# Sums of weight quarters on another engine, two products placed earlier, and the norm's scale applied on token rows

## The chip, the cores and the metric

The kernel runs as one program on one core of a Trainium2 chip. The metric is the device time of one execution in microseconds (us); before the change it is the median of three runs. The core has a matrix engine (TensorE, PE, whose weight loads are the row PEld), a vector engine (DVE), a scalar engine (ACT), GpSimd (POOL) and an engine that here only issues transfers (SyncE, SP). Transfers are DMAs; those issued by POOL stand in POOL's own instruction order, and an *accumulating* DMA adds what it moves to what the target holds.

## What is computed

The reference is a backbone of two layers that share their structure. Each layer has a feed-forward block, a mixer and a second feed-forward block, each between a norm that is scaled and shifted by a conditioning vector and a norm that is gated:

```python
def _layer(x, mod, lp, ctx):
    s0, c0, g0, s1, c1, g1, s2, c2, g2 = jnp.split(mod, N_MOD, axis=-1)
    h = _rms(x, lp["g_pre"][0]) * (1 + c0) + s0
    f = _swiglu(h, lp["w_ffn_gate"][0], lp["w_ffn_up"][0], lp["w_ffn_down"][0])
    x = x + 0.5 * g0 * _rms(f, lp["g_post"][0])
    ...

def _swiglu(h, wg, wu, wd):
    return (jax.nn.silu(h @ wg) * (h @ wu)) @ wd
```

The part left out is the mixer with `s1`, `c1`, `g1` and the second feed-forward block (FFN) with `s2`, `c2`, `g2`. `_rms(x, g)` is `x * rsqrt(mean(x*x) + 1e-6) * g`. There are 640 tokens (128 context, 512 latent) of width 1024; context and latent tokens have conditioning vectors of their own. The hidden width is 2816. Everything is float32.

## The kernel before

The 640 tokens are five tiles `t` of 128. A float32 matmul is made of three products of split operands: a weight slab `raw` is cast to `whi` by ACT (`split`, line 105) and the rest `wlo` is a subtraction on DVE (line 106); the three are `whi` by `hi`, `whi` by `lo`, `wlo` by `hi`. Up to six pairs `whi`, `wlo` exist at a time, so the splits can run that many products ahead of PE.

The blocks run in the order FFN, mixer, FFN, FFN, mixer, FFN. The first two FFNs are plain, the last two are *paired*: the gate and up matrices of a slab of hidden units are multiplied by a scheme with seven instead of eight block products. `seven` does this for one matrix of 1024 columns `w_pair`, in quarters `a11`, `a12`, `a21`, `a22` of 128x512. It loads `x` (`a11`, `a12`), `s` and `y` (`a21`, `a22`) by three DMAs on SP, adds `a22` to `s` and `a11` to `a21` by two accumulating DMAs from DRAM, and runs seven products of 12 matmuls each, 128x128 by 128x320, in line 671: B11, B21, T1, T3, T2, B22, T4. Between them `a11 += s` (after B11 has used `a11`) and `a12 += a11` (after B21 has used `a12`) are made by two more accumulating DMAs, from SBUF to SBUF; all four are issued by POOL in line 656. T2 and B22 read those sums. Two sets of buffers let the next `seven` load while one runs. A paired FFN starts with eight-product work on operands of `h` that are ready first, and then calls `seven` 20 times; `combine4` makes the last sum of quarters of `h`, an operand of T4, between the two.

Between two blocks the tokens are finished tile by tile: `postnorm` adds the gated output to `x`, `prenorm` computes `n = x * rs` (`rs` the reciprocal root mean square, a POOL power in line 304), `turn` transposes `n` on PE (line 334) and applies the affine map with the columns `A` and `B` as it leaves PSUM, half the pieces on DVE and half on ACT, and splits it. `rows` brings the gate row `G` onto all partitions: it transposes 16 rows on PE, writes them to DRAM (`gd`) and reads them back by four broadcasting DMAs into `P` tiles of 128x512. The transitions into the mixers and into the second plain FFN (three) have a plain target, the others a paired one.

A scheduler that simulates the engines' timelines sets the order of instructions on each engine from dependences and the order of the code; tiles of pools are given back when their last reader is through.

Of the kernel before, what the change touches and what calls it, by code (L numbers as in the profile page):

```python
# [2 lines left out]

# [30 lines left out]
class Builder:  # L34
# [227 lines left out]

    def rows(self, pg, f, pn):
        nc, v = self.nc, self.nc.vector
        s = self.tmp.tile([P, 512], F32, tag="tmp", name=self.nm("rows"))[:, :16]
# [4 lines left out]
        out = {}  # L272
        if pn:
            l, ph = pn
            a = self.sm.tile([P, 2, 8], F32, tag="acol", name=self.nm("acol"), bufs=2)
            for c in range(2):
                v.scalar_tensor_tensor(out=a[:, c], in0=self.mod[l]["m"][c][:, (3 * ph + 1) * 8:(3 * ph + 2) * 8],
                                       scalar=1.0, in1=self.mod[l]["gpre"][:, ph * 8:ph * 8 + 8], op0=ALU.add, op1=ALU.mult)
            out["A"] = [a[:, c] for c in range(2)]
            out["B"] = [self.mod[l]["m"][c][:, 24 * ph:24 * ph + 8] for c in range(2)]  # L280
        ps = self.tr()
        nc.tensor.transpose(ps[:16, :P], s, self.ident)
        g = self.tmp.tile([32, P], F32, tag="tmp", name=self.nm("grow"))
        nc.scalar.copy(g[:16], ps[:16, :P])  # L284
        d = self.dr.tile([2, 1024], F32, tag=self.nm("gd"), name=self.nm("gd"))
        nc.gpsimd.dma_start(d.rearrange("c (k p) -> (c k) p", p=P), g[:16])  # L286
        out["G"] = []
        for c in range(2):
            w = [self.P_(shape=[P, 512]) for _ in range(2)]
            for h in range(2):  # L290
                nc.gpsimd.dma_start(w[h], d[c:c + 1, 512 * h:512 * h + 512].to_broadcast([P, 512]))
            out["G"].append(w)
        return out


# [12 lines left out]

    def prenorm(self, t, x, R, hT):
        nc, v = self.nc, self.nc.vector  # L310
        n = self.bg.tile([P, 1024], F32, tag="bg", name=self.nm("n"))
        ss = self.S_()
        sq = nc.scalar.activation(n, x, AF.Square, scale=1.0 / 32.0, accum_out=ss)
        rs = self.rstd(ss)
        self.norm = (v.tensor_scalar(n, x, rs, None, ALU.mult), sq)

        def turn():
            self.turn(t, n, R, hT)

        (self.turns if t < 3 else self.late).append(turn)  # L320

# [4 lines left out]

    def turn(self, t, n, R, hT):
        nc, v = self.nc, self.nc.vector
        a, b = (R[k][0 if t == 0 else 1] for k in "AB")
        hs = []  # L330
        for q in range(2):
            ps = self.tr()
            for i in range(4):
                nc.tensor.transpose(ps[:, i * P:(i + 1) * P], n[:, (4 * q + i) * P:(4 * q + i + 1) * P], self.ident)
            h = n[:, q * 512:(q + 1) * 512].rearrange("p (k t) -> p k t", k=4)
            for i in range(4):
                k = slice(4 * q + i, 4 * q + i + 1)
# [6 lines left out]
            if not hT.paired:  # L344
                hi, lo = (z[q][:, :, t * P:(t + 1) * P] for z in hT.raw)
                d = self.split(hi, lo, h)
        if hT.paired:
            for c, n_, half, o in self.PIECES[t]:
                h, cs = [h[:, :, c:c + n_] for h in hs], slice(o, o + n_)
                d = self.quarters(hT, h, half, cs)  # L350
                if half:
                    self.todo.append(lambda h=h, cs=cs: self.combine(hT, h, cs))
            if t == 2:
                self.combos()
        if t < 3:
            self.turned = d

# [106 lines left out]
    def ffn(self, l, i, hT, ph, nxt, last, first=None):  # L464
        nc, A = self.nc, self.A
# [5 lines left out]
        for ch, n in enumerate(phases):  # L471
# [8 lines left out]
            for nh in range(2):  # L480
                ps = [self.mm() for _ in range(NT)]
                STG = min(n - 1, self.stage(self.STG[0], hTn)) if (final and nh == 1) else 0
                for jj in range(n - STG):
                    if last and final and nh == 0 and jj == 1:
                        w = self.W_()
                        self.xpre = [self.xp.tile([P, 1024], F32, tag="x", name=self.nm("x")) for _ in range(2)] + \
                            [self.bg.tile([P, 1024], F32, tag="bg", name=self.nm("x")) for _ in range(2)] + [w[:, :1024]]
                        for t in range(NT):
                            nc.sync.dma_start(self.xpre[t], self.xsrc[t])
                    if dram and final and nh == 0 and jj == 0:  # L490
                        part = self.new_part()
                        for t in range(NT):
                            nc.gpsimd.dma_start(part[t].whole, self.pd[t])
                    if final and nh == 0 and jj == 3:
                        R = self.rows((l, ph), 0.5, None if last else nxt)
# [77 lines left out]
    def paired(self, l, i, hT):  # L573
# [3 lines left out]
        w, ps = {}, {}  # L577
# [31 lines left out]
        for f in range(2):  # L609
# [1 line left out]
            first(f, 1, 1)  # L611
            product(f, 1)
            self.combos()
        self.combine4(hT)
        st = [self.rawp.tile([P, 1024], F32, tag="raw", name=self.nm("raw")) for _ in range(2)] + [self.P_(shape=[P, 512])]
        extra = self.seven(W[0, 1], st, hT.t)
        next(extra)
        yield hid[0]
        yield hid[1]
        big = self.big.tile([P, 5120], F32, tag="big", name=self.nm("raw2"))  # L620
        sets = [[big[:, o:o + 1024], big[:, o + 1024:o + 2048], big[:, o + 2048:o + 2560]] for o in (0, 2560)]
        for jp in range(1, NJ // 2):
            hid = [(self.P_(F32R), self.P_(F32R)) for _ in range(2)]
            for m in range(2):
                self.background(4 * jp + 2 * m)
                if extra:
                    g, extra = extra, None
                else:
                    g = self.seven(W[m, jp], sets[m], hT.t)
                    next(g)  # L630
                out = next(g)
                for done in g:
# [16 lines left out]

    def seven(self, src, st, T):
        nc, v, g = self.nc, self.nc.vector, self.nc.gpsimd
        x, y, s = st
        a11, a12, a21, a22 = x[:, :512], x[:, 512:], y[:, :512], y[:, 512:]
        add = lambda o, a: g.dma_start(o, a, accum_op=ALU.add)  # L656
        nc.sync.dma_start(x, src[:, :1024])
        nc.sync.dma_start(s, src[:, 1024:1536])
        self.last_slab = nc.sync.dma_start(y, src[:, 1024:])
# [15 lines left out]
        pa, pb = self.mm(), self.mm()  # L675
        product(pa, a11, "B11")
        nc.scalar.copy(o[0][0], pa[:, :TH])  # L677
        add(a11, s)
        product(pb, a12, "B21")
        v.tensor_tensor(o[0][0], o[0][0], pb[:, :TH], ALU.add)  # L680
        add(a12, a11)
        yield [(0, 0)]
        pe, pf = self.mm(), self.mm()
        product(pe, s, "T1")
# [286 lines left out]
    def mixer(self, l, hT):  # L971
# [31 lines left out]
        for nh in range(2):  # L1003
            ps = [self.mm() for _ in range(NT)]
            STG = self.stage(self.STG[1], hTn) if nh else 0
            for kc in range(KC - STG):
                if nh == 0 and kc == 2:
                    R = self.rows((l, 1), 1.0, (l, 2))
# [681 lines left out]
```

## Time and profile before

| | |
|---|---|
| median of three runs | 3324.78 us (3321.77 to 3325.75) |
| the profiled execution | 3323.45 us, span 3321.7 us |
| mean granted TensorE clock | 0.966 |
| PE, PEld busy | 94%, 87% of the span |
| DVE, ACT, POOL busy | 63%, 42%, 25% |
| DMA traffic | 466.04 MB, mean 140 GB/s |

The span is the time from the first to the last instruction in the trace of one execution; the execution's own time is 1.75 us more. Busy means that an instruction runs on an engine; instructions that issue a DMA, wait or branch are not counted as busy, except on POOL where issuing is shown. The clock is what the chip granted TensorE, as a share of the full 2.4 GHz; its other level is 1.2 GHz.

### The profile page before, as it was taken

What the parts mean: (1) busy time and instruction counts of PE and PEld (TensorE: products, weight loads), DVE (VectorE), ACT (ScalarE), POOL (GpSimd) and SP (SyncE); (2) the same over time, 40 slices, a digit from 0 to 9 for tenths busy, and PEclk for the clock granted to TensorE, in tenths of its full rate; (3) what the DMA queues carried; (4) which work ended last, traced back from release to release, by engine and by line L of the source; (5) the groups of instructions that cost most, each with busy time, mean ns of one, the idle gap of its engine ahead of it and who ended that gap; (6) DMA issues with size and microseconds to landing.
All of it is one profiled execution on the core that took longest, in us unless ns stands there. A gap on an engine that the chain in (4) does not pass through costs nothing. (4 is left out here: it accounts for less than half of the span.)

```text
span 3321.7 us, 51922 instructions
## 1 busy us (share of the span) xinstructions
PE 3105.8 (94%) x19501; PEld 2880.7 (87%) x19501; DVE 2088.2 (63%) x4256; ACT 1380.7 (42%) x3066; POOL 832.1 (25%) x1156
## 2 busy tenths in 40 slices
PE   8889999999999989999979898989999998898988
PEld 6888997888999889989778888877989997788887
DVE  7993775656544496737676745567575865755455
ACT  4222224565543343322343333446664334444333
POOL 2640002039520054210111112110693101112121
PEclk9999999999999999999989899999999999899999
DMA  6364544422542334655456767534226634566663
GB/s 240 124 207 128 164 147 135 100 70 61 113 133 76 122 115 151 195 130 180 139 161 187 183 161 158 165 110 90 69 66 163 198 107 143 146 185 155 161 150 127
DMA packets 174396, 466.04 MB, mean 140 GB/s; under 512 B 39120, under 2 KB 47840, under 8 KB 173120
## 3 DMA queue, kind: packets, MB, share of 16 engines
q1 hardware_dynamic: 131712, 369.71, 36.2%
q0 software_dynamic: 41712, 91.70, 12.9%
q8 instruction: 153, 2.51, 0.3%
q10 hardware_dynamic: 720, 1.31, 0.1%
q14 instruction: 99, 0.81, 0.1%
HBM read 386.70 MB, written 60.09 MB: 135 GB/s over the span
## 5 line engine op out<-in xcount | busy, mean ns | idle before, releaser
L106 DVE TENSOR_TENSOR wlo<-raw,whi 128x512 fp32r<-128x512 f32 x901 | 642.3, 720 | 639.1 <-ACT whi L105 630.5
L105 ACT CAST whi<-raw 128x512 fp32r<-128x512 f32 x901 | 544.5, 618 | 888.1 <-PE mm L100 352.7
L98 PE MATMUL mm<-h,whi 128*128 128x256 f32 (+1 forms) x2560 | 796.1, 313 | 7.2 <-ACT h L105 4.5
L100 PE MATMUL mm<-h,wlo 128*128 128x256 f32 (+1 forms) x2560 | 794.5, 311 | 5.0 <-DVE wlo L106 4.9
L99 PE MATMUL mm<-h,whi 128*128 128x256 f32 (+1 forms) x2560 | 795.3, 311 | 0.0
L98 PEld LDWEIGHTS mm<-h,whi 128*128 128x128 f32 x2560 | 488.6, 191 | 12.2 <-ACT h L105 4.9
L100 PEld LDWEIGHTS mm<-h,wlo 128*128 128x128 f32 x2560 | 489.3, 191 | 7.0 <-DVE wlo L106 6.9
L99 PEld LDWEIGHTS mm<-h,whi 128*128 128x128 f32 x2560 | 489.9, 191 | 1.8 <-issue 1.2
L99 PE MATMUL mm<-wlo,P 128*128 128x512 f32 x1015 | 395.9, 391 | 0.0
L98 PE MATMUL mm<-whi,P 128*128 128x512 f32 x1015 | 393.9, 391 | 1.8 <-DVE tmp L562 1.8
L100 PE MATMUL mm<-whi,P 128*128 128x512 f32 x1015 | 395.3, 390 | 0.0
L259 DVE SCALAR_TENSOR_TENSOR junk<-wmod,srows 128x1024 bf16<-128x1024 f32 x256 | 317.1, 1239 | 77.7 <-DMA wmod<-w_mod 76.5
L671 PE MATMUL mm<-hT,whi 128*128 128x320 f32 x1280 | 300.1, 324 | 55.5 <-ACT P L677 34.4
L671 PEld LDWEIGHTS mm<-hT,whi 128*128 128x128 f32 x1280 | 225.0, 199 | 63.3 <-ACT P L677 39.3
L671 PE MATMUL mm<-hB,whi 128*128 128x320 f32 x960 | 231.4, 331 | 33.4 <-ACT whi L105 31.6
L98 PEld LDWEIGHTS mm<-whi,P 128*128 128x128 f32 x1015 | 191.2, 188 | 42.1 <-DVE tmp L562 2.3
L100 PEld LDWEIGHTS mm<-whi,P 128*128 128x128 f32 x1015 | 191.2, 188 | 39.8
L99 PEld LDWEIGHTS mm<-wlo,P 128*128 128x128 f32 x1015 | 191.3, 188 | 39.3 <-DVE wlo L106 0.5
L671 PEld LDWEIGHTS mm<-hB,whi 128*128 128x128 f32 x960 | 173.1, 204 | 42.9 <-ACT whi L105 37.1
L671 PE MATMUL mm<-hT,wlo 128*128 128x320 f32 x640 | 203.0, 320 | 0.0
L286 POOL DMA_DIRECT2D gd<-grow x6 | 3.0, 506 | 673.2 <-ACT grow L284 673.2
L105 ACT CAST P<-tmp 128x384 fp32r<-128x384 f32 (+1 forms) x112 | 51.6, 461 | 283.9 <-DVE tmp L563 269.8
(394 smaller groups left out, 5489.9 us busy)
## 6 DMA issues: line engine op xcount, KB each, us to landing
wmod<-w_mod SPq DMA_DIRECT2D x128, 512.0 KB, 4.2
raw<-w_down SPq DMA_DIRECT2D x88, 512.0 KB, 3.7
raw<-w_pair SPq DMA_DIRECT2D x88, 512.0 KB, 5.4
raw<-w_in_fm SPq DMA_DIRECT2D x72, 512.0 KB, 3.6
raw<-w_gate SPq DMA_DIRECT2D x44, 512.0 KB, 3.7
raw<-w_up SPq DMA_DIRECT2D x44, 512.0 KB, 3.6
raw<-w_pair POOLq DMA_DIRECT2D x78, 256.0 KB, 4.3
raw<-raw POOLq DMA_DIRECT2D x78, 256.0 KB, 5.2
```

What stands on the lines that cost most here:

```text
L98: nc.tensor.matmul(ps, whi, ahi, start=first, stop=False)
L99: nc.tensor.matmul(ps, whi, alo, start=False, stop=False)
L100: nc.tensor.matmul(ps, wlo, ahi, start=False, stop=last)
L105: nc.scalar.copy(hi, src)
L106: return nc.vector.tensor_tensor(lo, src, hi.bitcast(F32), ALU.subtract)
L259: nc.vector.scalar_tensor_tensor(out=jk, in0=w, scalar=1.0, in1=rows[:, c], op0=ALU.mult, op1=ALU.mult, accum_out=m[:, c:c + 1])
L286: nc.gpsimd.dma_start(d.rearrange("c (k p) -> (c k) p", p=P), g[:16])
L671: nc.tensor.matmul(ps[:, :TH], w[:, cs], T[b][:, z, k], start=not more and k == e == 0, stop=k == 3 and e == 2, skip_group_check=more)
```

## The change

Three things change. First, in `seven` the two sums between the products become additions on POOL (`addp`); the two sums from DRAM stay DMAs. Second, the generator of the first `seven` of a paired FFN is advanced past its first two products before `combine4` is written, so that their code stands ahead of it. Third, for a plain target `rows` also turns the scale `A` into a token row: one transpose of 32 rows and one broadcasting DMA of 1 MB each for `G` and `A`, into `W` tiles; `prenorm` then applies `rs` and `A` to the token tile (DVE the first half; ACT `rs` and POOL `A` the second half), and the new `turn_plain` only adds `B`: for the first two tiles one DVE addition of four pieces and then the split; for the others ACT writes the high part with a bias and DVE the low part. The last FFN, which has no following block, has only `G` there.

```diff
     def rows(self, pg, f, pn, paired):
...
+            if paired:
+                a = self.sm.tile([P, 2, 8], F32, tag="acol", name=self.nm("acol"), bufs=2)
+                out["A"] = a = [a[:, c] for c in range(2)]
+            else:
+                n, a = 32, [s[:, 16 + 8 * c:24 + 8 * c] for c in range(2)]
...
+        nc.gpsimd.dma_start(d.rearrange("c (k p) -> (c k) p", p=P)[:n], g[:n])
+        if paired:
...
+        for key, r in (("G", 0), ("A", 2))[:2 if pn else 1]:
+            w = self.W_()
+            nc.gpsimd.dma_start(w[:, 0:2048], d[r:r + 2].rearrange("c x -> (c x)").unsqueeze(0).to_broadcast([P, 2048]))
+            out[key] = [[w[:, 1024 * i + 512 * h:1024 * i + 512 * h + 512] for h in range(2)] for i in range(2)]
         return out
...
-        self.norm = (v.tensor_scalar(n, x, rs, None, ALU.mult), sq)
+        if hT.paired:
+            self.norm = (v.tensor_scalar(n, x, rs, None, ALU.mult), sq)
+        else:
+            a = R["A"][0 if t == 0 else 1]
+            self.norm = (
+                v.scalar_tensor_tensor(out=n[:, :512], in0=x[:, :512], scalar=rs, in1=a[0], op0=ALU.mult, op1=ALU.mult),
+                nc.scalar.mul(n[:, 512:], x[:, 512:], rs))
+            self.last_n = nc.gpsimd.tensor_tensor(n[:, 512:], n[:, 512:], a[1], ALU.mult)
...
+    def turn_plain(self, t, n, R, hT):
...
+            if t < 2:
+                h = n[:, q * 512:(q + 1) * 512].rearrange("p (k t) -> p k t", k=4)
+                v.tensor_tensor(h, ps.rearrange("p (k t) -> p k t", k=4),
+                                B[:, 4 * q:4 * q + 4].unsqueeze(2).to_broadcast([P, 4, P]), ALU.add)
                 d = self.split(hi, lo, h)
...
+            for i in range(4):
+                o, b = ps[:, i * P:(i + 1) * P], B[:, 4 * q + i:4 * q + i + 1]
+                nc.scalar.activation(hi[:, i], o, AF.Identity, bias=b)
+                d = v.scalar_tensor_tensor(out=lo[:, i], in0=o, scalar=b, in1=hi[:, i].bitcast(F32),
+                                           op0=ALU.add, op1=ALU.subtract)
...
-        self.combine4(hT)
         st = [self.rawp.tile([P, 1024], F32, tag="raw", name=self.nm("raw")) for _ in range(2)] + [self.P_(shape=[P, 512])]
         extra = self.seven(W[0, 1], st, hT.t)
         next(extra)
+        extra = extra, next(extra), [next(extra)]
+        self.combine4(hT)
...
+        addp = lambda o, a: g.tensor_tensor(o, o, a, ALU.add)
...
-        add(a11, s)
+        addp(a11, s)
         product(pb, a12, "B21")
         v.tensor_tensor(o[0][0], o[0][0], pb[:, :TH], ALU.add)
-        add(a12, a11)
+        addp(a12, a11)
```

Where the instructions now stand shows in three places. The first is SP's order around the loads of the first `seven` in the first paired FFN: `P` is the tile of `s`, `raw` those of `x` and `y`, `wmod` weights of the conditioning, `w_down` of the FFN's second matrix. Before:

```order
L659 DMA raw_2709_17303<-w_pair 128x1024
L657 DMA raw_17295<-w_pair 128x1024
L659 DMA raw_17296<-w_pair 128x1024
L255 DMA wmod_17906<-w_mod 128x1024
L255 DMA wmod_17928<-w_mod 128x1024
L658 DMA P_17297<-w_pair 128x512
L255 DMA wmod_17960<-w_mod 128x1024
```

and now:

```order
L700 DMA raw_2711_17353<-w_pair 128x512
L701 DMA raw_2711_17353<-w_pair 128x1024
L699 DMA raw_17292<-w_pair 128x1024
L701 DMA raw_17293<-w_pair 128x1024
L700 DMA P_17294<-w_pair 128x512
L256 DMA wmod_17916<-w_mod 128x1024
L78 DMA raw_17906<-w_down 128x1024
```

The load of `s` has moved ahead of the two `wmod` loads that it followed. The second is POOL's order in the first `seven`s of the same FFN, before:

```order
L656 DMA raw_17296<-w_pair 128x512
L656 DMA P_17297<-w_pair 128x512
L656 DMA raw_17295<-P_17297 128x512
L656 DMA raw_17295<-raw_17295 128x512
L656 DMA raw_2709_17303<-raw_2709_17303 128x512 x2
L656 DMA raw_2709_17303<-w_pair 128x512
L656 DMA raw_2709_17303<-raw_2709_17303 128x512
L656 DMA raw_2709_17303<-w_pair 128x512
```

and now:

```order
L697 DMA raw_17293<-w_pair 128x512
L697 DMA P_17294<-w_pair 128x512
L698 TENSOR_TENSOR raw_17292<-raw_17292,P_17294 128x512
L698 TENSOR_TENSOR raw_17292<-raw_17292 128x512
L698 TENSOR_TENSOR raw_2711_17353<-raw_2711_17353 128x512 x2
L697 DMA raw_2711_17353<-w_pair 128x512
L698 TENSOR_TENSOR raw_2711_17353<-raw_2711_17353 128x512
L697 DMA raw_2711_17353<-w_pair 128x512
```

The DMAs whose source is SBUF have become additions in the same places; those from `w_pair` have stayed. The third is POOL's order at the first transition (FFN to mixer), where `s` are the `rs` of a tile, `x` the sum into the residual. Before:

```order
L304 TENSOR_TENSOR s_5143<-s_5141,mhalf 128x1
L304 TENSOR_TENSOR s_5153<-s_5151,mhalf 128x1
L304 TENSOR_TENSOR s_5188<-s_5186,mhalf 128x1
L304 TENSOR_TENSOR s_5198<-s_5196,mhalf 128x1
L304 TENSOR_TENSOR s_5255<-s_5253,mhalf 128x1
L454 TENSOR_TENSOR x_5251<-part_2606,x_5251 128x512
L304 TENSOR_TENSOR s_5266<-s_5264,mhalf 128x1
L304 TENSOR_TENSOR s_5323<-s_5321,mhalf 128x1
L454 TENSOR_TENSOR x_5319<-part_2606,x_5319 128x512
```

and now:

```order
L315 TENSOR_TENSOR s_5138<-s_5136,mhalf 128x1
L315 TENSOR_TENSOR s_5148<-s_5146,mhalf 128x1
L315 TENSOR_TENSOR s_5185<-s_5183,mhalf 128x1
L333 TENSOR_TENSOR n_5143<-n_5143,W_4827 128x512
L315 TENSOR_TENSOR s_5195<-s_5193,mhalf 128x1
L333 TENSOR_TENSOR n_5190<-n_5190,W_4827 128x512
L315 TENSOR_TENSOR s_5248<-s_5246,mhalf 128x1
L492 TENSOR_TENSOR x_5244<-part_2606,x_5244 128x512
L315 TENSOR_TENSOR s_5259<-s_5257,mhalf 128x1
L315 TENSOR_TENSOR s_5312<-s_5310,mhalf 128x1
L333 TENSOR_TENSOR n_5254<-n_5254,W_4827 128x512
L492 TENSOR_TENSOR x_5308<-part_2606,x_5308 128x512
```

A multiply of `n` by the scale row `W` now stands among the powers and the sums for `x`, once for each token tile.

## Rows read from the trace of the kernel before

**Rows 1.** The page, engines and costliest group: busy us, share, instructions; group: busy, mean ns.

```profile
PE 3105.8 (94%) x19501; PEld 2880.7 (87%) x19501; DVE 2088.2 (63%) x4256; ACT 1380.7 (42%) x3066; POOL 832.1 (25%) x1156
...
L106 DVE TENSOR_TENSOR wlo<-raw,whi 128x512 fp32r<-128x512 f32 x901 | 642.3, 720 | 639.1 <-ACT whi L105 630.5
```

**Rows 2.** Waits of PE, whole span: us in total, times, longest.

```profile
PE mm L671 <- ACT whi L105: 50.8, 20, 7.4
PE mm L671 <- ACT P L677: 34.4, 17, 3.9
PE mm L334 <- DVE n L315: 29.8, 6, 8.8
```

**Rows 3.** Windows, six stretches of `seven`: us, then busy (instructions) by engine, PEclk, DMA.

```profile
1701.50:1771.70 70.20, 53.48 (x314) 51.58 (x313) 50.55 (x99) 26.38 (x56) 12.09 (x14) 0.85 0.63 155
1816.50:1941.30 124.80, 107.83 (x649) 102.47 (x648) 84.10 (x172) 51.72 (x113) 26.21 (x32) 0.92 0.74 179
1999.40:2120.50 121.10, 104.72 (x648) 101.61 (x647) 72.97 (x149) 53.35 (x117) 28.64 (x35) 0.93 0.64 140
2850.80:2916.40 65.60, 52.25 (x314) 50.17 (x313) 43.46 (x83) 26.99 (x57) 12.22 (x14) 0.87 0.58 135
2960.90:3078.80 117.90, 102.92 (x648) 100.13 (x647) 72.25 (x145) 51.40 (x114) 26.09 (x31) 0.95 0.73 170
3138.00:3255.10 117.10, 102.90 (x649) 100.17 (x648) 66.76 (x134) 52.00 (x115) 26.87 (x34) 0.94 0.68 157
sum 616.70, PE 524.11 PEld 506.13 DVE 390.10 ACT 261.84 POOL 132.13; mean PE 87.35 PEld 84.36 DVE 65.02 ACT 43.64 POOL 22.02
```

**Rows 4.** Windows, line 671 alone, a stretch without a stall.

```profile
2961.00:2982.00 21.00, 21.00 (x144) 20.90 (x143) 1.00 0.87 241
```

**Rows 5.** Waits of ACT, whole span: us in total, times, longest.

```profile
ACT whi L105 <- DMA raw<-raw: 234.3, 60, 7.5
```

**Rows 6.** The page, DMA issues: count, KB each, median us to landing.

```profile
raw<-w_pair POOLq DMA_DIRECT2D x78, 256.0 KB, 4.3
raw<-raw POOLq DMA_DIRECT2D x78, 256.0 KB, 5.2
```

**Rows 7.** Timeline of POOL and ACT in one `seven`: start, us, instruction, [idle before <-releaser].

```profile
2012.12 0.86 POOL L656 DMA_DIRECT2D raw<-raw  x1 [1.38 <-DVE wlo L106]
...
2020.18 0.86 POOL L656 DMA_DIRECT2D raw<-raw  x1
...
2019.76 0.62 ACT L105 CAST whi<-raw 128x512 fp32r<-128x512 f32 x1 [3.64 <-DMA raw<-raw]
...
2026.76 0.62 ACT L105 CAST whi<-raw 128x512 fp32r<-128x512 f32 x1 [6.01 <-DMA raw<-raw]
```

**Rows 8.** Timeline of SP and POOL at the last sum of h.

```profile
1701.87 0.38 SPq L658 DMA_DIRECT2D P<-w_pair  x1
...
1707.49 0.86 POOL L656 DMA_DIRECT2D P<-w_pair  x1 [14.15 <-DMA P<-w_pair]
```

**Rows 9.** Waits of PE, 1701.5 to 1716.5 and 2850.8 to 2863.

```profile
PE mm L671 <- ACT whi L105: 9.7, 2, 7.4
...
PE mm L671 <- ACT whi L105: 6.7, 1, 6.7
```

**Rows 10.** Line 454's group (ns min/median/max), then POOL and DVE timelines beside it.

```profile
L454 POOL TENSOR_TENSOR x<-part,x x15: 1264/1391/3938, 540.3 to 2816.7; 128x512 f32<-128x512 f32 x15
...
551.33 3.94 POOL L454 TENSOR_TENSOR x<-part,x 128x512 f32<-128x512 f32 x1 [0.83 <-ACT part L453]
...
552.24 1.29 DVE L106 TENSOR_TENSOR wlo<-raw,whi 128x512 fp32r<-128x512 f32 x2
...
2176.16 1.79 DVE L106 TENSOR_TENSOR wlo<-raw,whi 128x512 fp32r<-128x512 f32 x1
```

**Rows 11.** Groups of lines 315 and 453: ns min/median/max.

```profile
L315 DVE TENSOR_SCALAR n<-x,s x25: 744/753/755, 533.4 to 2826.9; 128x1024 f32<-128x1024 f32 x25
...
L453 ACT ACTIVATE part<-part,s x15: 722/723/750, 539.5 to 2815.9; 128x512 f32<-128x512 f32 x15
```

More of the change, by code (lines that the diff above doesn't have):

```diff
@@ L261, in mod_tile, with rows @@
         nc.vector.tensor_tensor(m, m, self.mod[l]["b"][:, col:col + 1].to_broadcast([P, 2]), ALU.add)
-    def rows(self, pg, f, pn):
+    def rows(self, pg, f, pn, paired):
         nc, v = self.nc, self.nc.vector
-        s = self.tmp.tile([P, 512], F32, tag="tmp", name=self.nm("rows"))[:, :16]
+        s = self.tmp.tile([P, 512], F32, tag="tmp", name=self.nm("rows"))[:, :32]
         l, ph = pg
@@ L272, in rows @@
         out = {}
+        n = 16
         if pn:
             l, ph = pn
-            a = self.sm.tile([P, 2, 8], F32, tag="acol", name=self.nm("acol"), bufs=2)
+            if paired:
[3 more added lines that the diff above has]
+                n, a = 32, [s[:, 16 + 8 * c:24 + 8 * c] for c in range(2)]
             for c in range(2):
-                v.scalar_tensor_tensor(out=a[:, c], in0=self.mod[l]["m"][c][:, (3 * ph + 1) * 8:(3 * ph + 2) * 8],
+                v.scalar_tensor_tensor(out=a[c], in0=self.mod[l]["m"][c][:, (3 * ph + 1) * 8:(3 * ph + 2) * 8],
@@ L278, in rows @@
                                        scalar=1.0, in1=self.mod[l]["gpre"][:, ph * 8:ph * 8 + 8], op0=ALU.add, op1=ALU.mult)
-            out["A"] = [a[:, c] for c in range(2)]
             out["B"] = [self.mod[l]["m"][c][:, 24 * ph:24 * ph + 8] for c in range(2)]
         ps = self.tr()
-        nc.tensor.transpose(ps[:16, :P], s, self.ident)
+        nc.tensor.transpose(ps[:n, :P], s[:, :n], self.ident)
         g = self.tmp.tile([32, P], F32, tag="tmp", name=self.nm("grow"))
-        nc.scalar.copy(g[:16], ps[:16, :P])
@@ L285, in rows @@
[L285 to L292, printed above, removed]
+        nc.scalar.copy(g[:n], ps[:n, :P])
+        d = self.dr.tile([4, 1024], F32, tag=self.nm("gd"), name=self.nm("gd"))
@@ new lines, in rows @@
+        nc.gpsimd.dma_start(d.rearrange("c (k p) -> (c k) p", p=P)[:n], g[:n])
+        if paired:
+            out["G"] = []
+            for c in range(2):
+                w = [self.P_(shape=[P, 512]) for _ in range(2)]
+                for h in range(2):
+                    nc.gpsimd.dma_start(w[h], d[c:c + 1, 512 * h:512 * h + 512].to_broadcast([P, 512]))
+                out["G"].append(w)
+            return out
+        for key, r in (("G", 0), ("A", 2))[:2 if pn else 1]:
+            w = self.W_()
+            nc.gpsimd.dma_start(w[:, 0:2048], d[r:r + 2].rearrange("c x -> (c x)").unsqueeze(0).to_broadcast([P, 2048]))
+            out[key] = [[w[:, 1024 * i + 512 * h:1024 * i + 512 * h + 512] for h in range(2)] for i in range(2)]
@@ L314, in prenorm @@
         rs = self.rstd(ss)
-        self.norm = (v.tensor_scalar(n, x, rs, None, ALU.mult), sq)
+        if hT.paired:
[6 more added lines that the diff above has]
+            self.last_n = nc.gpsimd.tensor_tensor(n[:, 512:], n[:, 512:], a[1], ALU.mult)
         def turn():
-            self.turn(t, n, R, hT)
+            (self.turn if hT.paired else self.turn_plain)(t, n, R, hT)
         (self.turns if t < 3 else self.late).append(turn)
@@ L343, in turn @@
             hs.append(h)
-            if not hT.paired:
-                hi, lo = (z[q][:, :, t * P:(t + 1) * P] for z in hT.raw)
-                d = self.split(hi, lo, h)
[L347 to L354, printed above, removed]
+        for c, n_, half, o in self.PIECES[t]:
+            h, cs = [h[:, :, c:c + n_] for h in hs], slice(o, o + n_)
+            d = self.quarters(hT, h, half, cs)
+            if half:
+                self.todo.append(lambda h=h, cs=cs: self.combine(hT, h, cs))
+        if t == 2:
+            self.combos()
+        if t < 3:
+            self.turned = d
+    def turn_plain(self, t, n, R, hT):
+        nc, v = self.nc, self.nc.vector
+        B = R["B"][0 if t == 0 else 1]
+        for q in range(2):
+            ps = self.tr()
+            for i in range(4):
+                kc = 4 * q + i
+                nc.tensor.transpose(ps[:, i * P:(i + 1) * P], n[:, kc * P:(kc + 1) * P], self.ident)
+            hi, lo = (z[q][:, :, t * P:(t + 1) * P] for z in hT.raw)
+            if t < 2:
+                h = n[:, q * 512:(q + 1) * 512].rearrange("p (k t) -> p k t", k=4)
+                v.tensor_tensor(h, ps.rearrange("p (k t) -> p k t", k=4),
+                                B[:, 4 * q:4 * q + 4].unsqueeze(2).to_broadcast([P, 4, P]), ALU.add)
+                d = self.split(hi, lo, h)
+                continue
+            for i in range(4):
+                o, b = ps[:, i * P:(i + 1) * P], B[:, 4 * q + i:4 * q + i + 1]
+                nc.scalar.activation(hi[:, i], o, AF.Identity, bias=b)
+                d = v.scalar_tensor_tensor(out=lo[:, i], in0=o, scalar=b, in1=hi[:, i].bitcast(F32),
+                                           op0=ALU.add, op1=ALU.subtract)
         if t < 3:
@@ L494, in ffn @@
                     if final and nh == 0 and jj == 3:
-                        R = self.rows((l, ph), 0.5, None if last else nxt)
+                        R = self.rows((l, ph), 0.5, None if last else nxt, not last and hTn.paired)
                     whi, wlo = next(it)
@@ L626, in paired @@
                 if extra:
-                    g, extra = extra, None
+                    g, out, head = extra
+                    extra = None
                 else:
-                    g = self.seven(W[m, jp], sets[m], hT.t)
+                    g, head = self.seven(W[m, jp], sets[m], hT.t), []
                     next(g)
-                out = next(g)
-                for done in g:
+                    out = next(g)
+                for done in itertools.chain(head, g):
                     for f, h in done:
@@ L1007, in mixer @@
                 if nh == 0 and kc == 2:
-                    R = self.rows((l, 1), 1.0, (l, 2))
+                    R = self.rows((l, 1), 1.0, (l, 2), hTn.paired)
                 whi, wlo = next(it)
```

1 line of the change is left out of this document (added).

## Prediction, written before the changed kernel ran

> **What bounds the kernel now.** I read the page first: TensorE (PE) is busy 3105.8 of 3321.7 us [rows 1]. What can be won is its idle time and the time in which its clock is low. The waits of PE say where the idle time lies: in line 671, the matmuls of the paired matrices' products, and at the turns of the normed tokens [rows 2]. So I cut out the six stretches in which the products of `seven` run and read them as windows [rows 3]: 616.70 us, PE busy 524.11, idle 92.6. At the full clock 144 such matmuls take 21.0 us [rows 4], 0.1458 us each, so 12 of a product take 1.75 us and the 84 of one `seven` 12.25. The 3222 matmuls of the stretches [rows 3] would take 469.8 us; that PE is busy 524.1 there, at a granted clock of 0.85 to 0.95 [rows 3], is 54.3 us for the lower of the two levels, 1.2 GHz, to which the clock drops around the stalls. Idle and clock together, 147 us, is the most that the stretches can give.
>
> What ends the idle time: ACT's casts of `whi` wait 234.3 us, 60 times, for the DMA that adds SBUF to SBUF [rows 5]. One `seven` shows how [rows 7]: POOL issues `a11+=s` at 2012.12 and the cast that reads it starts at 2019.76, 7.6 us later; `a12+=a11` is issued at 2020.18 and its cast starts at 2026.76, 6.6 us later. The median landing of such a DMA is 5.2 us [rows 6]. The two sums in series make 14.2 us, and PE wants the next operands every 12.25 us: 1.95 us are missing for each of the 38.4 `seven`s of the stretches (3222/84), 75 us. The idle time agrees: 92.6, less 9.7 and 6.7 us that stand at another place (below), is 76.2.
>
> **The change, part by part.** *The two sums on POOL.* It removes two DMAs from each `seven` (78 in the page [rows 6], two more under another name) and adds as many POOL additions 128x512. POOL runs that form already, in line 454: 1264 at least, 1391 median, 3938 ns at most [rows 10]. Two in series are 2.8 us at the median, and 7.9 us at the worst. Both ends lie under 12.25 us, so the chain that made PE wait is gone for either price; before it, POOL waits for the accumulating DMA `s+=a22`, which lands in 4.3 us [rows 6]: 0.86 us issue [rows 7] + 4.3 + 2.8 = 8.0 us, still under 12.25. What is late next: the first operands of a stretch, the loads of the sets, DVE's `wlo`. I have no row that shows these waits without the DMA; between 0 and the whole 76.2 I take a third, 26 us, as an estimate: six stretch starts of about 3 us, and single stalls of the size that remain beside the DMA. That is -50 us. Removing the stalls also removes drops of the clock. I scale the 54.3 us with the idle time.
>
> What the additions cost elsewhere: DVE shares the time with them. In the one place of before where an `L106` subtraction ran beside such an addition and was hurt, it took 1.79 instead of the mean of 0.72 us, 1.07 us lost; at another place DVE did its subtractions in 0.65 us each and the addition took 3.94 [rows 1, 10]. So the price for DVE is 0 to 1.07 us a sum; I take the middle, 0.54. 77 sums (2 x 38.4) make 41 us, and DVE goes from 390.1 [rows 3] to 431 us in stretches that last about 520: cover enough, since DVE has 89 us left. The addition waits on POOL behind the accumulating DMAs and these behind it, both in order; POOL's time of 132 us in the stretches [rows 3] loses 77 x 0.86 = 66 and gains 77 x 1.39 = 107.
>
> Here a rule of the Trainium skill speaks against the change: SBUF — State Buffer, section "Who interferes with whom", says that DVE and GpSimd share a pair of ports under an exclusive lock, and that a DVE instruction with two SBUF inputs contends with a GpSimd instruction that reads SBUF; the one that issues second is fully blocked. The rows show now one side hurt and now the other, as that has it, but by 1.07 and not by the other's whole length where DVE lost [rows 10]. By the rows a sum costs DVE 0.54 us on the middle; by the rule up to the whole 1.39, which is the first rival.
>
> *Two products ahead of the last sum of h.* In the trace PE already runs the 24 matmuls of B11 and B21 there and then waits. The stalls are 9.7 us (two waits) and 6.7 us in the second paired ffn [rows 9]. They end with `whi` cast from `s`, and `s` came late: its load was issued at 1701.87 on SP behind two `wmod` loads, POOL's accumulating DMA followed at 1707.49 after 14.15 us of waiting [rows 8]. In the new order the load of `s` stands ahead of the `wmod` loads, and its buffer is one that PE gave back long before. So this stall goes, though not for the reason that the change's words give. What is late next is DVE's sums of h, which T1 and T4 read; I have no row without the late `s`, so, between 0 and 16.4, I leave 3 us in each of the two places: 16.4 to 6, -10 us.
>
> So idle goes from 92.6 to 32 us, 35%; the clock's 54.3 us to 18.8, -35.5 us.
>
> *Norm scale on token rows.* Three plain transitions are touched. On each late token tile the path was one DVE multiply of 128x1024, 0.75 us; it becomes a half on DVE beside an ACT multiply (0.72 us for 128x512 in line 453) and then a POOL multiply 128x512 of 1.26 to 3.94 us [rows 10, 11]. That is 0.72 + 1.26 - 0.75 = +1.2 up to +3.9 us before the transposes of a tile. PE waits for this `n` 29.8 us in six waits now, 8.8 the longest [rows 2], so there is no cover for the last tiles. Behind it the turn saves: DVE and ACT no longer scale, and the first tiles add B in one instruction for four pieces. Fifteen POOL multiplies are new, and they stand on POOL ahead of the next tile's sum for `x`. Four broadcasts `P<-gd` become two of 1 MB; they are issued some us before the first use. I take +2 us a transition, +6; bounds -9 (the shorter turn brings back as much as the longest of the six waits, 8.8) and +23 (two late tiles of 3.9 us on each transition).
>
> **Sum:** -50 -10 -35.5 +6 = -89.5. From the profiled run's 3323.45 us this is 3234. The median of the runs shown is 3324.78, 1.3 us more, so I predict 3235.
>
> **The rivals.**
>
> 1. *DVE becomes the bound of the products* because every sum keeps it off for the whole of 1.39 us. Then DVE needs 390 + 77 x 1.39 = 497 us; in the first, second and fourth stretch (7.5, 15.4 and 7.5 sums) it needs 61, 105.5 and 54 us where PE needs 45.8, 94.6 and 45.8: 34 us more than my sum has. 3235 + 34 = about 3269. For it: the 1.79 us row; against: 0.65 us rows beside 3.94 [rows 10]. 17%.
> 2. *The loads take the place of the sums.* Each set's `s+=a22` and `a21+=a11` stay DMAs, in POOL's order behind the additions. If half of the 76.2 us stays, and with it half of the clock's loss: -38 -10 -27 +6 = -69, 3256. For it: two sets only, and loads of 4.3 us [rows 6] that follow SP's; against: 8.0 of 12.25 us by the chain above. 12%.
> 3. *The second part doesn't do what it says and gives nothing*, since the products already stood ahead and `s` is late for another reason: 10 us and a sixth of the clock's gain less, 3235 + 16 = 3251. It is part of my range. 10%.
> 4. *All stalls and drops go:* 3325 - 147 + 6 = 3184. 5%.
> 5. *Slower: POOL becomes the bound.* When DVE's stream holds the additions off, each takes 3.94 us as in the worst row [rows 10]. Then POOL has per `seven` two sums (7.9), two issues (1.7) and, if it waits for the two accumulating DMAs one after the other, 8.6 us: 18.2 us where a `seven` takes 616.7/38.4 = 16.1 now. 2.1 x 38.4 = +81, with the transitions 3412. It is slower from about 2.9 us a sum ((16.1 - 10.3)/2). For it: DVE is 65% busy in the stretches [rows 3]; against: the median is 1.39 us, and the two DMAs are issued for two products that PE wants at different times. 6%.
>
> **How the numbers follow.** My forecast, 3205 to 3249, has 45%; the rivals 17, 12, 10, 5 and 6%; no change within 0.2% (6.6 us, about what a measurement of this kernel can tell) 5%, if gains and losses of the parts cancel. Range: 3190 to 3285 holds the forecast and rivals 1 to 3, and leaves out most of rivals 4 and 5, the unchanged case and the tails of 1 and 2, some 18%. Faster by over 0.2%: 0.88; within: 0.05; slower: 0.07.
>
> **What the new profile would show.** Right: no DMA `raw<-raw` and 78 to 80 additions on POOL of 1.3 to 2 us; ACT's casts not waiting for DMAs in the stretches; PE idle there about 32 us and the clock at 0.96 or more; the stalls of 7.4 and 6.7 us shrunk to about 3; the waits for `n` at the turns grown by some us. Rival 1: PE waiting for `wlo`, DVE over 90% busy in the stretches, `L106` at 1.2 us or more. Rival 2: casts waiting for `raw<-w_pair`. Rival 5: POOL additions near 3.9 us. What would make it wrong at all: if the idle time that I put down to the DMAs is that of a chain which also passes DVE, and stays when the DMAs are gone.

## Result and profile after

The changed kernel takes 3207.41 us (median of four runs, 3204.23 to 3211.27) where the kernel before, run beside it, takes 3325.27: a ratio of 0.9643 (95% interval 0.9623 to 0.9664), 118 us less. Forecast were 3235 us in a range of 3190 to 3285. All times below are medians of four or five executions; one of the five of `one_dma` took 9797 us, and that kernel's ratio leaves it out. The profiled execution has a span of 3203.3 us and a mean granted clock of 0.983 (0.966 before).

The page of the changed kernel, engines, the costliest group of DVE, POOL's additions and the accumulating DMAs that are left; they answer to [rows 1, 6]:

```profile
PE 3056.2 (95%) x19501; PEld 2840.4 (89%) x19501; DVE 2172.3 (68%) x4262; ACT 1386.1 (43%) x3075; POOL 897.8 (28%) x1162
...
L107 DVE TENSOR_TENSOR wlo<-raw,whi 128x512 fp32r<-128x512 f32 x901 | 684.8, 764 | 451.6 <-ACT whi L106 445.5
...
L698 POOL TENSOR_TENSOR raw<-raw 128x512 f32<-128x512 f32 x78 | 124.1, 1591 | 180.1 <-DVE wlo L107 177.2
...
raw<-w_pair POOLq DMA_DIRECT2D x78, 256.0 KB, 4.5
```

The row `raw<-raw` is gone. PE is busy 50 us less for the same 19501 matmuls, which is clock; DVE is busy 84 us more for six more instructions.

Where the 118 us went is read from six windows again, this time cut at the first and the last of the products' matmuls, which are 336 or 672 in each stretch in both kernels (the cut of [rows 3] left 24 of each out). First the kernel before, then the changed one; the columns are those of [rows 3]:

```profile
1701.50:1781.74 80.24, 63.49 (x365) 60.19 (x364) 58.50 (x115) 31.06 (x67) 12.96 (x15) 0.87 0.66 166
...
sum 653.78, PE 561.16 PEld 540.25 DVE 418.14 ACT 279.38 POOL 135.28; mean PE 93.53 PEld 90.04 DVE 69.69 ACT 46.56 POOL 22.55
```

```profile
1697.60:1766.60 69.00, 61.67 (x374) 57.52 (x373) 68.86 (x121) 31.86 (x68) 14.64 (x12) 0.98 0.57 162
1799.30:1908.70 109.40, 102.90 (x680) 99.84 (x679) 103.27 (x184) 56.71 (x122) 37.49 (x33) 1.00 0.70 190
1961.60:2066.40 104.80, 101.91 (x680) 101.38 (x679) 92.81 (x154) 57.09 (x121) 39.46 (x40) 0.98 0.59 152
2791.30:2848.30 57.00, 52.44 (x344) 50.58 (x344) 56.17 (x99) 30.11 (x64) 14.87 (x12) 1.00 0.51 147
2887.60:2989.20 101.60, 101.09 (x680) 99.84 (x679) 91.33 (x156) 56.37 (x121) 34.20 (x32) 1.00 0.66 178
3042.20:3142.30 100.10, 100.10 (x680) 99.83 (x679) 83.77 (x140) 56.57 (x119) 34.85 (x34) 1.00 0.64 177
sum 541.90, PE 520.10 PEld 508.99 DVE 496.20 ACT 288.71 POOL 175.51; mean PE 86.68 PEld 84.83 DVE 82.70 ACT 48.12 POOL 29.25
```

The stretches give 111.9 of the 118.4 us by which the spans differ: 70.8 us of idle time (92.6 before, 21.8 now) and 41.1 us of PE's busy time at a higher clock. In the last stretch there is nothing left: PE is busy all of its 100.1 us, and eight `seven`s at 12.25 us are 98.0. The first stretch has another bound: DVE is busy 68.86 of 69.00 us. The other 6.5 us lie ahead of the first stretch (3.9) and in the work between stretches.

The waits of PE in the changed kernel, the answer to [rows 2]:

```profile
PE mm L352 <- DVE n L327: 15.6, 3, 9.0
PE mm L713 <- DVE wlo L107: 12.9, 13, 2.1
...
PE mm L380 <- DVE n L331: 9.0, 2, 7.1
...
PE mm L380 <- POOL n L333: 5.6, 3, 3.5
```

The products wait 12.9 us for `wlo` where they waited 50.8 and 34.4 us behind ACT; line 352 is the turn for a paired target and line 380 the new one.

### The profile page after: what moved, and what is told of

Its sections match the earlier page's. It is cut to its first block, busy times and chain, and to the rows that moved or that the text cites. A ratio compares the mean times of both kernels' runs of the same rounds, so it can differ in the third digit from the quotient of the medians.

```text
span 3203.3 us, 51877 instructions
## 1 busy us (share of the span) xinstructions
PE 3056.2 (95%) x19501; PEld 2840.4 (89%) x19501; DVE 2172.3 (68%) x4262; ACT 1386.1 (43%) x3075; POOL 897.8 (28%) x1162
## 4 chain that ended last, share of the span: by engine, by line
PE 70%; DVE 13%; POOL 6%; issue 5%; DMA 3%; ACT 2%; SPq 0%; DVEq 0%; POOLq 0%; ACTq 0%
PE mm L99 17%; PE mm L100 17%; PE mm L101 17%; PE mm L713 12%; DVE wlo L107 3%; DVE junk L260 2%; POOL H L1313 1%; POOL s5t L1311 1%; POOL s5t L1312 1%; POOL s5t L1310 1%; PE mm L1545 1%; PE mm L1534 1%; DMA raw<-w_pair 1%; DVE P L107 1%; DMA pd<-put 1%
## 5 line engine op out<-in xcount | busy, mean ns | idle before, releaser
L107 DVE TENSOR_TENSOR wlo<-raw,whi 128x512 fp32r<-128x512 f32 x901 | 684.8, 764 | 451.6 <-ACT whi L106 445.5
L713 PE MATMUL mm<-hT,whi 128*128 128x320 f32 x1280 | 284.7, 310 | 7.5 <-ACT P L719 3.7
L713 PEld LDWEIGHTS mm<-hT,whi 128*128 128x128 f32 x1280 | 213.9, 188 | 10.1 <-ACT P L719 4.2
L713 PE MATMUL mm<-hB,whi 128*128 128x320 f32 x960 | 213.1, 312 | 0.0
L698 POOL TENSOR_TENSOR raw<-raw 128x512 f32<-128x512 f32 x78 | 124.1, 1591 | 180.1 <-DVE wlo L107 177.2
```

What stands on the lines that cost most here:

```text
L107: return nc.vector.tensor_tensor(lo, src, hi.bitcast(F32), ALU.subtract)
L698: addp = lambda o, a: g.tensor_tensor(o, o, a, ALU.add)
L713: nc.tensor.matmul(ps[:, :TH], w[:, cs], T[b][:, z, k], start=not more and k == e == 0, stop=k == 3 and e == 2, skip_group_check=more)
```

## The experiments

**Each part alone or undone.** The first four ran on one chip, where the kernel before took 3328.64 us.

*The sums back to DMAs, the rest as changed* (`no_sums`):

```diff
-        addp = lambda o, a: g.tensor_tensor(o, o, a, ALU.add)
+        addp = lambda o, a: g.dma_start(o, a, accum_op=ALU.add)
```

> The changed kernel with its two additions on POOL turned back into accumulating DMAs; the other two parts stay. Theory (two sums by DMA in series, 14.2 us, against 12.25 us of matmuls): the stalls of about 2 us per seven and the low clock come back; the milestones of the two traces put 112 of the 118 us into the stretches of seven, and of these some 20 belong to the place of the last sum of h, so about 90 us are lost: 3297 us. Rival (a large share comes from the second part, which lets the splits run ahead): under 3270 us.

3302.37 us, ratio 0.9914 (0.9896 to 0.9932). ACT's casts wait for the DMAs as in [rows 5]:

```profile
ACT whi L106 <- DMA raw<-raw: 228.8, 59, 7.3
```

By the two ratios (0.9914 against 0.9643) the sums carry some 90 us of the changed kernel's gain; the other two parts by themselves give 26.

*The sums alone in the kernel before* (`sums_only`):

```diff
-        add(a11, s)
+        addp(a11, s)
...
-        add(a12, a11)
+        addp(a12, a11)
```

> The kernel before with nothing but the two additions on POOL. Theory: 3325 - 90 = 3235 us; the two stalls at the last sum of h stay (9.7 and 6.7 us). If the three parts add up, this and the run without the sums share the 118 us. Rival (POOL's additions need the freed tiles of the other parts, or only work with them): above 3270 us.

3218.55 us, ratio 0.9662 (0.9641 to 0.9682): 110 us, more than expected. 110 and 26 are 18 us more than both together bring: what the other parts remove is partly hidden once the sums are on POOL.

*The second part undone* (`no_ahead`):

```diff
+        self.combine4(hT)
         st = [self.rawp.tile([P, 1024], F32, tag="raw", name=self.nm("raw")) for _ in range(2)] + [self.P_(shape=[P, 512])]
         extra = self.seven(W[0, 1], st, hT.t)
         next(extra)
-        extra = extra, next(extra), [next(extra)]
-        self.combine4(hT)
+        extra = extra, next(extra), []
```

> The changed kernel with the second part undone: combine4 is written first, then the loads of the first seven, then its products. Theory (the late load of s was the stall): the two stalls come back, 16 us of idle time less the 3 to 4 that are left there now, and some 8 us of low clock: 3227 us. Rival (the scheduler hoists them anyway, the second part gives nothing): 3207 us.

3212.68 us, ratio 0.9644 (0.9627 to 0.9661), no difference from the changed kernel's 0.9643 that these runs can tell; the profiled span is 5.3 us longer. The time is 14 us under the theory's and nearer the rival's. The stalls themselves came back all the same, as the waits of PE in its first and fourth stretch and SP's order in the timeline show:

```profile
PE mm L713 <- ACT whi L106: 5.9, 2, 5.8
...
PE mm L713 <- ACT whi L106: 5.2, 1, 5.2
```

```profile
1697.21 1.94 SPq L256 DMA_DIRECT2D wmod<-w_mod  x2
1699.24 0.38 SPq L700 DMA_DIRECT2D P<-w_pair  x1
```

The load of `s` is again behind two `wmod` loads, PE waits 11 us in two places, and the first stretch still takes the 69.0 us that it takes without the stall.

*The third part undone* (`no_rows`): the kernel before with the first two parts.

```diff
-        addp = lambda o, a: g.dma_start(o, a, accum_op=ALU.add)
+        addp = lambda o, a: g.tensor_tensor(o, o, a, ALU.add)
...
+        extra = extra, next(extra), [next(extra)]
+        self.combine4(hT)
```

The first pair of lines stands for the edit of `sums_only`; `rows`, `prenorm` and `turn` are those of the kernel before.

> The kernel before with the first two parts, without the token rows of the third. Theory from the milestones (the first two plain transitions ended 4 us earlier, the third the same): 3211 to 3213 us. Rival (the prediction's own term, +6 us for the third part): 3201 us. The waits of PE for n and for h at the three plain transitions tell them apart: 25 us in all before.

3209.62 us, ratio 0.9636 (0.9618 to 0.9654), the changed kernel's within the intervals; its span is 3.4 us longer than the changed kernel's. PE's waits at the three transitions sum to 26.2 us here and to 19.3 in the changed kernel. So the third part does not cost. Behind the second part its gain is too small for these runs. Without the second part it shows: `no_ahead`, which has the first and the third, took 3210.37 to 3213.54 us, and `sums_only`, on the same chip, 3217.54 to 3219.79, a difference of 5.9 us between the medians.

**What the second part gives.** The loads ahead of `combine4`, the products behind it (`load_early`, beside a kernel before of 3330.58 us, as the next three):

```diff
         next(extra)
-        extra = extra, next(extra), [next(extra)]
         self.combine4(hT)
+        extra = extra, next(extra), []
```

> The changed kernel with the loads of the first seven ahead of combine4, but its products written behind it. Theory (what the second part gives is the early load of s): the same as the changed kernel within 4 us, 3207 to 3211 us, and no wait of 7 us there. Rival (the place of the products in the code gives it): about as without the second part, 3227 us.

3203.48 us, ratio 0.9619 (0.9599 to 0.9638), 3.5 us under the range expected; by the ratios no difference from the changed kernel that these runs can tell. SP's order, and PE's wait for `whi` in the first stretch:

```profile
1683.18 0.37 SPq L700 DMA_DIRECT2D P<-w_pair  x1
1701.68 0.33 SPq L256 DMA_DIRECT2D wmod<-w_mod  x1
...
PE mm L713 <- ACT whi L106: 0.4, 1, 0.4
```

The place of the products in the code gives no gain; the early load of `s` removes the stall by itself.

**Is the series of sums the cause?** The second sum as a DMA, the first on POOL (`one_dma`):

```diff
         addp(a11, s)
...
-        addp(a12, a11)
+        add(a12, a11)
```

> The changed kernel with the second sum, a12 += a11, as an accumulating DMA and only the first on POOL. Theory of the chain: 1.6 + about 7 us in series stay under the 12.25 us of a seven, so hardly any stall returns, and DVE loses only 40 sums instead of 80: 3200 to 3212 us. Rival (each DMA among the sums stalls PE by itself, not their length in series): half of the loss returns, about 3250 us.

3244.99 us, ratio 0.9744 (0.9724 to 0.9763): the rival's number. Over a third of the sums' gain is lost although 1.6 + 7 us lie well under 12.25. The four long stretches take 108.6 to 115.5 us for their eight `seven`s, 13.6 to 14.4 us each, and ACT waits for `raw<-raw` 32 times:

```profile
1969.00:2084.50 115.50, 106.17 (x681) 103.05 (x680) 82.42 (x154) 55.28 (x121) 36.32 (x40) 0.97 0.62 153
...
3078.10:3186.70 108.60, 102.82 (x680) 99.98 (x680) 76.57 (x140) 53.89 (x119) 32.05 (x34) 1.00 0.68 173
...
ACT whi L106 <- DMA raw<-raw: 134.5, 32, 7.6
```

The timelines of ACT and of POOL in its last stretch show why:

```profile
3107.58 0.62 ACT L106 CAST whi<-raw 128x512 fp32r<-128x512 f32 x1 [1.55 <-DMA raw<-raw]
...
3121.93 0.62 ACT L106 CAST whi<-raw 128x512 fp32r<-128x512 f32 x1 [4.70 <-DMA raw<-raw]
```

```profile
3111.82 1.48 POOL L698 TENSOR_TENSOR raw<-raw 128x512 f32<-128x512 f32 x1 [2.75 <-DVE wlo L107]
3115.91 0.89 POOL L697 DMA_DIRECT2D raw<-w_pair  x1 [2.62 <-DVE P L733]
3116.49 1.22 POOL L697 DMA_DIRECT2D raw<-raw  x1
```

The cast of `a12` of one `seven` starts at 3107.58. Behind it in ACT's order are the casts of the next `seven`; their `wlo` lets POOL add at 3111.82, 4.2 us later. The addition ends at 3113.30, but the DMA stands in POOL's order behind the accumulating DMA for another set, which is issued at 3115.91, after a wait that the trace puts down to a DVE sum of products (line 733); it goes out at 3116.49, and the cast of this `a12` starts at 3121.93. The whole round takes 14.35 us, not 8.6, and that is more than 12.25. The 3.2 us from 3113.30 to 3116.49 belong to POOL's order; without them the round would be 11.2 us, but no run took this DMA out of that order. The same round in the kernel before, from the `seven` of [rows 7] on, POOL and then ACT:

```profile
2030.40 0.86 POOL L656 DMA_DIRECT2D raw<-raw  x1 [4.95 <-DVE wlo L106]
...
2037.31 0.86 POOL L656 DMA_DIRECT2D raw<-raw  x1 [0.28 <-issue]
```

```profile
2036.89 0.62 ACT L105 CAST whi<-raw 128x512 fp32r<-128x512 f32 x1 [3.87 <-DMA raw<-raw]
...
2043.18 0.62 ACT L105 CAST whi<-raw 128x512 fp32r<-128x512 f32 x1 [5.31 <-DMA raw<-raw]
```

From the cast at 2026.76 [rows 7] to that at 2043.18 are 16.4 us, of which 3.6 lie between the cast of `a12` and the next `a11+=s` at 2030.40. From a cast to its like is the pace of the work whatever sets it; here the lines show what sets it, since what ends the waits on the way is a `wlo` or a DMA of the round itself, and never PE. The pace agrees with the mean of the stretches, 616.7/38.4 = 16.1 us.

**What the additions cost DVE.** Both sums on DVE (`dve_sums`):

```diff
-        addp = lambda o, a: g.tensor_tensor(o, o, a, ALU.add)
+        addp = lambda o, a: v.tensor_tensor(o, o, a, ALU.add)
```

> The changed kernel with both sums of a seven on DVE instead of POOL. In the changed kernel DVE is busy 496 us in the stretches, 78 more than before, for 80 sums that it does not run: 0.98 us a sum. Theory (the POOL additions hold DVE off, and DVE is the bound of the first stretch of each paired FFN): a sum on DVE itself takes about 0.69 us, so DVE falls by some 20 us in the stretches and the sums no longer wait for an engine change: 3195 to 3203 us. Rival (DVE is not the bound, its order is what counts, and a sum in it delays the subtractions behind): 3207 to 3220 us.

3195.36 us, ratio 0.9595 (0.9578 to 0.9612). The page's engines, the first of the six windows and their sum, and the group of the sums:

```profile
PE 3064.8 (96%) x19501; PEld 2851.5 (89%) x19501; DVE 2145.3 (67%) x4342; ACT 1389.3 (43%) x3075; POOL 776.1 (24%) x1082
...
1702.30:1766.40 64.10, 59.48 (x376) 56.40 (x375) 63.27 (x125) 31.27 (x68) 5.18 (x6) 1.00 0.61 173
...
sum 532.30, PE 519.91 PEld 511.91 DVE 464.77 ACT 292.23 POOL 74.69; mean PE 86.65 PEld 85.32 DVE 77.46 ACT 48.70 POOL 12.45
```

```profile
L698 DVE TENSOR_TENSOR raw<-raw x78: 674/684/693, 1701.3 to 3115.6; 128x512 f32<-128x512 f32 x78
```

DVE is busy 31 us less in the stretches than in the changed kernel, although 69 of the 80 sums run on it there. The price of an addition on POOL is read over the whole execution, where all 80 fall. Here DVE is busy 2145.3 us, of which the sums are 80 x 0.684 = 54.7; the rest, 2090.6, against the changed kernel's 2172.3 makes 81.7/80 = 1.02 us that an addition on POOL costs DVE. `sums_only` and the kernel before, both with 4256 DVE instructions, differ in the sums alone:

```profile
PE 3068.5 (95%) x19501; PEld 2855.7 (89%) x19501; DVE 2173.2 (68%) x4256; ACT 1389.4 (43%) x3066; POOL 880.8 (27%) x1156
```

That is (2173.2 - 2088.2)/80 = 1.06 us. About 1 us, then, and more than the 0.684 that the sum costs DVE when DVE does it. The first stretch, which DVE filled, is 64.1 us long instead of 69.0, so DVE was its bound.

One place of the changed kernel, POOL and then DVE:

```profile
2909.07 1.47 POOL L698 TENSOR_TENSOR raw<-raw 128x512 f32<-128x512 f32 x1 [3.72 <-DVE wlo L107]
...
2914.23 1.61 POOL L698 TENSOR_TENSOR raw<-raw 128x512 f32<-128x512 f32 x1
```

```profile
2909.30 1.79 DVE L107 TENSOR_TENSOR wlo<-raw,whi 128x512 fp32r<-128x512 f32 x1
...
2913.77 2.10 DVE L262 TENSOR_TENSOR mod<-mod,bmod 128x2 f32<-128x2 f32 x1
```

Line 262 adds two columns, 0.16 us at the median; it takes 2.10 here and ends with POOL's addition, within 0.03 us. That the addition held it is read from the two ends; it had started 0.46 us earlier.

*The first sum on DVE, the second on POOL* (`sum_split`):

```diff
-        addp(a11, s)
+        v.tensor_tensor(a11, a11, s, ALU.add)
```

> The changed kernel with the first sum, a11 += s, on DVE and the second on POOL. Theory (POOL additions hold DVE off by 0.98 us, a sum on DVE takes 0.69): between the changed kernel and the one with both on DVE, 3200 to 3206 us. Rival: 3207 us or more.

3202.23 us, ratio 0.9617 (0.96 to 0.9633), between the two, though its interval meets both of theirs.

*POOL work that nobody waits for.* The last four kernels ran beside a kernel before of 3329.92 us. `dummy_add` is `dve_sums` with five additions of 128x96 on POOL behind each sum, `dummy_set` with one of 128x1 and five memsets; both leave the output alone.

```diff
         addp(a11, s)
+        [g.tensor_tensor(self.scr, a11[:, 96 * i:96 * i + 96], s[:, 96 * i:96 * i + 96], ALU.add) for i in range(5)]
...
         addp(a12, a11)
+        [g.tensor_tensor(self.scr, a12[:, 96 * i:96 * i + 96], a11[:, 96 * i:96 * i + 96], ALU.add) for i in range(5)]
```

> The kernel with both sums on DVE (3195 us), and behind each sum five POOL additions of 128x96 that read the tiles just summed and write a scratch tile which nobody reads; no engine waits for them except that a buffer is given back after them. Theory (a POOL instruction that reads SBUF holds DVE off): DVE is busy 70 to 90 us more in the stretches than the 465 us of the kernel with sums on DVE, over their 532 us, and the time is 3215 to 3245 us. Rival (DVE's longer rows in the changed kernel come from elsewhere): DVE stays at 465 us, 3195 us.

```diff
         addp(a11, s)
+        [g.tensor_tensor(self.scr[:, :1], a11[:, :1], s[:, :1], ALU.add)] + [g.memset(self.scr, 0.0) for _ in range(5)]
```

and the same behind the second sum.

> The same with, behind each sum, one POOL addition of 128x1 and five POOL memsets of 128x96, which keep POOL busy without reading SBUF. Theory (what is read counts): DVE's time rises by less than 15 us and the time is 3192 to 3203 us. Rival (a busy POOL, its writes or its order count): like the run with the additions, above 3210 us.

3225.72 us (0.9692, 0.9678 to 0.9706) and 3197.5 us (0.9606, 0.9593 to 0.9619). The sums of the six windows, `dummy_add` and then `dummy_set`:

```profile
sum 564.70, PE 531.80 PEld 520.48 DVE 504.86 ACT 284.59 POOL 310.13; mean PE 88.63 PEld 86.75 DVE 84.14 ACT 47.43 POOL 51.69
```

```profile
sum 532.20, PE 520.61 PEld 513.23 DVE 461.40 ACT 289.10 POOL 171.44; mean PE 86.77 PEld 85.54 DVE 76.90 ACT 48.18 POOL 28.57
```

In `dummy_set` POOL is busy 97 us more in the stretches than in `dve_sums` (over the whole execution 78 us of memsets and 46 us of additions of one column), and DVE is where it was, 461 beside 465 us, and the time too. In `dummy_add` POOL is busy 235 us more and DVE 40 us, and the additions that read 96 columns take 0.72 us at the median, 0.38 at the least. So POOL work that hardly reads costs DVE nothing here and POOL work that reads does. The two loads on POOL are not equally long; no run made them so. The 40 us were expected at 70 to 90, and the time's 30 us are not DVE's alone: with POOL busy 310 of 565 us the accumulating DMAs in its order come late, and ACT's casts wait 39.0 us for `raw<-w_pair` where they waited 5.7 in `dve_sums`.

**Put together.** Both sums on DVE and the order of `load_early` (`best`), with the changed kernel once more (`changed_again`):

```diff
-        addp = lambda o, a: g.tensor_tensor(o, o, a, ALU.add)
+        addp = lambda o, a: v.tensor_tensor(o, o, a, ALU.add)
...
-        extra = extra, next(extra), [next(extra)]
         self.combine4(hT)
+        extra = extra, next(extra), []
```

> Both sums on DVE, the loads of the first seven ahead of combine4 and its products behind it. Each of the two edits was a few us below the changed kernel (3195 and 3203 us against 3207). If they add up: 3190 to 3194 us. If the products' place doesn't matter: 3195 us.

> The changed kernel once more, unchanged, on the same chip as the version with both edits, so that the two can be set against each other: 3205 to 3211 us.

3192.41 us (0.9594, 0.9581 to 0.9607) beside 3209.11 us (0.9638, 0.9624 to 0.9651) for the changed kernel: 17 us, half a per cent, better than both kernels. What of it is `load_early`'s edit can't be told from `dve_sums` alone (0.9595).

## Why the prediction came out

**Where the time lies: right.** The idle time of the products ended with the SBUF-to-SBUF DMAs, and the clock's loss went with it. Of idle time the sum took away 60 us (50 and 10), and 70.8 went; of the clock's loss it took 35.5, and PE's busy time fell by 41.1. The sum (89.5 us) falls 29 us short of what the span lost (118.4). Some 16 of these are idle time and clock that it kept as what comes late next (32 us of idle time kept, 21.8 left). The other 12.5 lie outside the stretches, where it added 6 us and 6.5 went.

**Two sums in series against 12.25 us: the comparison was wrong, the end right.** 14.2 - 12.25 = 1.95 us met the idle time of 2 us per `seven` by chance. The round that repeats has also the casts and `wlo` of the next `seven`, 3.6 to 4.2 us, and POOL's order: 16.4 us in the kernel before. That is 4 us over 12.25, which is the idle time and the clock's loss together ((92.6 + 54.3)/38.4 = 3.8 us), not the idle time alone. By the prediction's comparison `one_dma` would have lost nothing; it lost some 34 us (0.9744 against 0.9643). With both sums as additions the round is short enough for either way of reckoning, so the step gave the right answer for the changed kernel.

**The price of a POOL addition: mis-sized.** For DVE it was put at 0.54 us, the middle of 0 and 1.07; it is about 1.0 (1.02 and 1.06 in the two ways above), near the upper end. The trace of the kernel before had more rows for it than the one that the prediction took for the only one: beside line 454's additions three subtractions of line 106 were drawn out, to 1.79, 1.38 and 1.13 us (at 2176, 2801 and 1653 us). On POOL an addition takes 1.59 us on average, not 1.39. So DVE is busy 496 of 542 us in the stretches, where on the same cut 418 of before and the sum's 41 would have made 459. That cover was nearly gone: the first stretch of each paired FFN is filled by DVE now (68.86 of 69.00 and 56.17 of 57.00 us). The first rival had the right places, first, second and fourth stretch, and two of its signs came: PE waits for `wlo`, and DVE is 92% busy. Its size was too high, 390 + 107 = 497 us on the cut of [rows 3], which is 418 + 107 = 525 on this one; and its added 34 us did not come, because it put them on top of the idle time that the sum kept, while PE's idle time in all six stretches is 21.8 us. The Trainium skill's rule on the shared ports, SBUF — State Buffer, "Who interferes with whom", by which a DVE instruction with two SBUF inputs contends with a GpSimd instruction that reads SBUF and not with one that only writes it, agrees with `dummy_add` and `dummy_set` in kind (DVE 40 us more with reads, 3 us less with memsets). In size DVE lost about 1.0 of an addition's 1.59 us; what became of the rest the runs don't show.

**Two products ahead: the stall right, its worth wrong.** The late load of `s` was the cause, as said: `load_early` shows that the load alone does it, and `no_ahead` brings load and stall back. But the 10 us and a share of the clock were counted as if nothing else bound the stretch. With the sums on POOL DVE fills it. On the sums alone the part is worth 9 us: `no_rows` took 3206.78 to 3212.82 us and `sums_only`, on the same chip, 3217.54 to 3219.79. On top of the third part it is worth nothing by the ratios of `no_ahead` and the changed kernel, 5 us by their spans. Rival 3, by which the part gives nothing, was nearer to its worth in the changed kernel, though not for its reason. In the kernel with DMAs the other two parts give 26 us together; how much of that is this one was not run apart.

**Token rows: sign wrong, inside the bounds.** +6 us was forecast for the transitions, because `n` would come later. It did not, as far as PE's waits show: at the three places PE waited 15.1 us for `n` before and waits 14.6 now (5.6 for POOL's multiply, 9.0 for DVE's half). The waits behind the turn, for `h` and a `wlo`, shrank from 10.6 to 4.8 us, which the sum did not count as a saving. Together that is 25.7 us before and 19.3 now, and `no_ahead` beside `sums_only` puts the part's gain at 5.9 us.

Rivals 2 and 5 did not come: casts wait 3.0 us for `raw<-w_pair` and 4.7 for `P<-w_pair` in the changed kernel, and no addition of a `seven` took more than 2.27 us.

## What to carry to other kernels

When work repeats, compare the whole round, from an instruction to its like in the next turn and through every in-order engine on the way, with the time that the bounding engine needs; a part of the round that happens to agree with the idle time proves little. An SBUF-to-SBUF addition that is given to POOL to spare DVE can cost DVE more than doing it there (about 1.0 against 0.68 us here): price the neighbour's loss, and try the direct way. And a stall that is removed is worth only what the next bound of the same stretch leaves of it.

## What was not expected of the hardware

A DVE addition of two columns, 0.16 us at the median, took 2.10 us in one place and ended with a POOL addition, so a short instruction may be held as long as a large one. The 78 us of POOL memsets beside DVE's work in `dummy_set` cost it nothing that shows (DVE 2145.5 us over the whole execution, 2145.3 in `dve_sums`), while additions that read tiles of the same size cost DVE 40 us in `dummy_add`.
